# Moving weight splits behind short chains, more room for split weights, and a longer lag of the first layer's down products

## The chip, the cores and the metric

The kernel runs on one core of a Trainium2 chip. The metric is the device time of one execution in microseconds (us). Engines are named as in the profile: PE (TensorE) multiplies matrices, DVE (VectorE) and ACT (ScalarE) work element by element, POOL (GpSimd) and SP (SyncE) do small rest work and issue DMAs.

## The reference

A decoder trunk of two layers on one sequence of 256 tokens, width 1024, all in float32:

```python
for i in range(2):
    h = rms_norm(x, norm_mix_g[i])
    x = x + (nsa_mixer(h, ...) if i == 0 else diff_mixer(h, ...))
    h = rms_norm(x, norm_ffn_g[i])
    u = conv3(h @ ffn_w_up[i]) + ffn_conv_b[i]        # causal, per channel; 1024 -> 2 x 2816
    gate, val = split(u)
    x = x + (silu(gate) * val) @ ffn_w_down[i]        # 2816 -> 1024
return rms_norm(x, final_norm_g)
```

`nsa_mixer` is a sparse attention with 16 heads in 4 groups. K and V of 32-token blocks are compressed by a small network, `gelu(blocks @ w1) @ w2`; each head mixes three softmaxes (over the compressed blocks, the selected blocks and a window) by gates, and an output product with `nsa_w_out` follows. `diff_mixer` has 8 heads with two softmaxes each, `p0 - lam * p1`, a norm per head and the output product.

## The kernel before, in words

**Weights.** Every weight is read once. The host lays them out as units of 128 x 1024 (or 1120) float32 in the order of use. `Stream.load` (L76) brings one to three units in one DMA on SP into a `raw` tile (three buffers). `Stream.split` (L94) makes of each unit a high part `hi`, cast on ACT (L113), and a rest `lo = raw - hi` on DVE (L116). A product is three matmuls: hi by x-high, hi by x-low and lo by x-high, where x itself is split into `xhi` and `xlo` (L186, L187). Split units live in a pool of six (`spl`), or in a place named by `S.place`. `S.fill(n)` splits ahead until n units are ready, `S.next()` takes one. So the 199 splits are background work on ACT and DVE that must stay ahead of PE, and they share these two queues with the short chains of the layers.

**Order.** The text of the kernel gives each engine's instructions, and the framework's scheduler settles the order within each engine's queue. An engine runs its queue in that order; one that waits holds up those behind it. `keep_in_program_order` pins an instruction, which `S.pin` did for one fill.

**First attention, `nsa` (L270).** K, V and q projections, `kbuild` (L467, key casts into the tiles `KK`, `KK2`), `blocks` (L371, the block diagonal of the compression), `cmp_mm` (L395, compression's first product into `cm`), then `cmp_out` (L406), a generator in four steps: copy `hs` on ACT (L409); transposes `ph`, copy `hx` (L415); GELU in `h` (L418 to L421); product `pk` (L441), for K (0) and for V (1). Then a loop over eight pairs of heads: `scores` (L541) with row minima, exponentials and scaling of `p` on DVE (L606), the next q projection, `transposes` (L617, tiles `ta`, `tw`, copies `va`, `vw`), `pv` (L634). The output product `oproj` (L667) runs in pieces; its last piece ends in `residual` (L265): add to `xT`, split into `xhi` and `xlo`, square.

**FFN, `ffn` (L889), twice.** 22 pairs of units: `up(p)` (L944, 48 matmuls into `u`), `conv(p)` (L964: scale `us`, two shifted sums, silu, product, split into `hh` and `hl`, L980 and L982), and `down(p - LAG)` (L922, into `acc`) two pairs behind. `norm_stats` (L204) gives the norm's factors; its diagonal `dg` feeds a small product.

**Second attention, `diff` (L723).** Per head `s_scores`, `s_trans`, `s_pv` and `s_out`, which ends in `doh` (high part on ACT, L829; low part on DVE, L830), read by the output product `dop`.

The change touches `group_plan` (L52), `Stream.split`, `split_tile`, `norm_stats`, `residual`, `nsa`, `diff`, `ffn` and the units' order in the host's packing.

## Time and profile before

| | |
|---|---|
| median of 3 runs | 661.22 us (661.07 to 662.81) |
| the profiled execution's own time | 662.8 us |
| its span in the trace | 661.0 us |
| mean granted clock of PE | 0.992 |
| matmuls on PE | 5026 |
| weights and other reads from memory | 109.27 MB |

The span runs from the first to the last instruction in the trace; the execution's own time holds 1.8 us more around it. Busy time of an engine is the time in which the trace shows it at work. A wait is idle time of an engine, put down to the instruction that ended it.

### The profile page before, as it was taken

To read this page: it belongs to the slowest core of one execution; us is meant where nothing else is said; L and a number is where in the kernel's file an instruction comes from. 1 tells how busy PE (TensorE), PEld (TensorE's weight loads), DVE (VectorE), ACT (ScalarE), POOL (GpSimd) and SP (SyncE) were. 2 spreads that over 40 slices of the span, in tenths; PEclk is the share of its full clock that TensorE was granted. 3 is DMA by queue.
4 is the path that set the end of the run, shared out by engine and by line. 5 is a ranking of instruction groups with operands and counts; after the bars stand their busy time and mean duration, and the time that the engine had idled before them with its cause. 6 is when DMAs were issued, how large, how long until landed. Compare 5 with 4: busy or idle time off the path is not lost.

```text
span 661.0 us, 12566 instructions
## 1 busy us (share of the span) xinstructions
PE 641.6 (97%) x5026; PEld 612.2 (93%) x5026; DVE 513.7 (78%) x990; ACT 413.8 (63%) x818; POOL 27.6 (4%) x39
## 2 busy tenths in 40 slices
PE   8999899999999999999999999999999999999994
PEld 8989798989999999999998899989999999999993
DVE  6899799859867777788859479865987777779664
ACT  7698787658655555567636568645665555558343
POOL 3200000000000000000002000000100000000002
PEclk9999799999999999999999999999999999999998
DMA  8967211124554555546622645720855554555301
GB/s 306 284 252 281 102 65 64 64 97 181 202 190 178 180 178 176 178 178 243 231 89 100 243 152 172 258 97 13 306 191 192 192 190 172 183 180 182 114 1 64
DMA packets 15770, 111.12 MB, mean 168 GB/s; under 512 B 1976, under 2 KB 3512, under 8 KB 5976
## 3 DMA queue, kind: packets, MB, share of 16 engines
q1 hardware_dynamic: 14976, 109.43, 46.5%
q8 instruction: 39, 0.64, 0.4%
q0 software_dynamic: 448, 0.37, 0.3%
q10 hardware_dynamic: 288, 0.52, 0.2%
q14 instruction: 19, 0.16, 0.1%
HBM read 109.27 MB, written 1.05 MB: 167 GB/s over the span
## 4 chain that ended last, share of the span: by engine, by line
PE 61%; issue 24%; DVE 8%; ACT 2%; POOL 1%; DMA 1%; SPq 1%; POOLq 0%; ACTq 0%; DVEq 0%
PE u L954 35%; PE acc L938 10%; PE acc L918 9%; PE dv L247 3%; DVE lo L116 3%; PE dqk L236 2%; PE dop L236 2%; ACT dp L263 1%; DMA raw<-wts 1%; DVE dp L789 1%; POOL dssq L816 1%; DVE dp L262 0%; DVE dp L788 0%; DVE cv L973 0%; DVE dos L820 0%
## 5 line engine op out<-in xcount | busy, mean ns | idle before, releaser
L113 ACT CAST hi<-raw 128x1024 fp32r<-128x1024 f32 (+2 forms) x199 | 202.4, 1045 | 98.6 <-PE u L954 55.8
L116 DVE TENSOR_TENSOR lo<-raw,hi 128x1024 fp32r<-128x1024 f32 (+2 forms) x199 | 239.6, 1222 | 14.5 <-ACT hi L113 14.0
L954 PE MATMUL u<-xhi,lo 128*128 128x256 f32 x704 | 198.6, 282 | 0.0
L954 PE MATMUL u<-xlo,hi 128*128 128x256 f32 x704 | 197.7, 281 | 0.9 <-DVE xlo L187 0.9
L954 PE MATMUL u<-xhi,hi 128*128 128x256 f32 x704 | 198.5, 282 | 0.0
L954 PEld LDWEIGHTS u<-xlo,hi 128*128 128x128 f32 x704 | 132.7, 188 | 1.8 <-DVE xlo L187 1.1
L954 PEld LDWEIGHTS u<-xhi,hi 128*128 128x128 f32 x704 | 132.7, 189 | 0.8 <-ACT xhi L186 0.2
L954 PEld LDWEIGHTS u<-xhi,lo 128*128 128x128 f32 x704 | 132.5, 188 | 0.0
L973 DVE SCALAR_TENSOR_TENSOR cv<-us,cs,cv 128x255 f32<-128x255 f32 (+1 forms) x176 | 74.6, 479 | 4.2 <-ACT cv L971 3.7
L966 DVE TENSOR_TENSOR us<-u,rrs 128x512 f32<-128x512 f32 x44 | 30.4, 690 | 53.4 <-PE u L954 53.3
L971 ACT ACTIVATE cv<-us,cs 128x256 f32<-128x256 f32 x88 | 48.1, 593 | 13.4 <-DVE us L966 13.3
L938 PE MATMUL acc<-hl,hi 128*128 128x256 f32 x176 | 49.7, 283 | 1.1 <-DVE hl L982 1.1
L938 PE MATMUL acc<-hh,lo 128*128 128x256 f32 x176 | 49.7, 282 | 0.0
L938 PE MATMUL acc<-hh,hi 128*128 128x256 f32 x176 | 49.6, 282 | 0.0
L980 ACT CAST hh<-cv 128x256 fp32r<-128x256 f32 x44 | 17.8, 406 | 44.3 <-DVE cv L978 44.3
L236 PE MATMUL dqk<-xhi,hi 128*128 128x256 f32 x128 | 37.1, 290 | 0.0
L236 PE MATMUL dqk<-xhi,lo 128*128 128x256 f32 x128 | 36.0, 282 | 0.0
L236 PE MATMUL dqk<-xlo,hi 128*128 128x256 f32 x128 | 36.0, 281 | 0.0
L938 PEld LDWEIGHTS acc<-hl,hi 128*128 128x128 f32 x176 | 33.2, 189 | 1.3 <-DVE hl L982 1.3
L938 PEld LDWEIGHTS acc<-hh,hi 128*128 128x128 f32 x176 | 33.3, 189 | 0.0
L938 PEld LDWEIGHTS acc<-hh,lo 128*128 128x128 f32 x176 | 33.3, 189 | 0.0
L976 ACT ACTIVATE cv<-cv 128x256 f32<-128x256 f32 x44 | 18.4, 417 | 20.6 <-DVE cv L973 20.6
(242 smaller groups left out, 1266.3 us busy)
## 6 DMA issues: line engine op xcount, KB each, us to landing
raw<-wts SPq DMA_DIRECT2D x40, 1536.0 KB, 6.6
raw<-wts SPq DMA_DIRECT2D x34, 1024.0 KB, 5.0
raw<-wts SPq DMA_DIRECT2D x7, 512.0 KB, 4.8
raw<-wts SPq DMA_DIRECT2D x2, 1120.0 KB, 7.8
db<-bib SPq DMA_DIRECT2D x8, 192.0 KB, 3.6
xT<-xin SPq DMA_DIRECT2D x4, 256.0 KB, 4.3
raw<-wts SPq DMA_DIRECT2D x2, 256.0 KB, 4.1
tail<-fng SPq DMA_DIRECT2D x1, 512.0 KB, 6.5
```

Source lines behind the costliest of these rows:

```text
L113: cast = nc.scalar.copy(hi[:, q], r[:, q])
L116: nc.vector.tensor_tensor(lo[:, q], r[:, q], hi[:, q].bitcast(F32), op=OP.subtract)
L236: nc.tensor.matmul(dst, w[:, kt * P : (kt + 1) * P], x[:, kt, :], start=kt == 0 and i == 0, stop=kt == KT - 1 and i == 2, skip_group_check ...
L247: nc.tensor.matmul(dst, x[:, kt, q * P : (q + 1) * P], w[:, k * cols : (k + 1) * cols], start=kt == 0 and i == 0, stop=kt == KT - 1 and i ...
L918: nc.tensor.matmul(acc[q][c // 512][:, c % 512 : c % 512 + d - c], x[:, qs], w[:, c:d], start=p == 0 and i == 0, stop=p == NPAIR - 1 and i ...
L938: nc.tensor.matmul(acc[dt // 2][:, dt % 2, :], w[:, dt * P : (dt + 1) * P], x, start=p == 0 and i == 0 and dt % 2 == 0, stop=p == NPAIR - ...
L954: nc.tensor.matmul(ps[:, b, :], w[:, kt * P : (kt + 1) * P], x[:, kt, :], start=kt == 0 and b == 0 and i == 0, stop=kt == KT - 1 and i == ...
L966: nc.vector.tensor_tensor(us, ps, rr.unsqueeze(1).to_broadcast([P, 2, T]), op=OP.mult)
L971: nc.scalar.activation(cv[:, b, :], us[:, b, :], AF.Identity, bias=w[3], scale=w[2])
L973: nc.vector.scalar_tensor_tensor(cv[:, b, sft:], us[:, b, : T - sft], w[2 - sft], cv[:, b, sft:], op0=OP.mult, op1=OP.add)
L976: nc.scalar.activation(cv[:, 0, :], cv[:, 0, :], AF.Silu)
L980: nc.scalar.copy(hh, h)
```

## The change

Five things change together.

- `with tc.issue_after(ins):` ties the instructions that a block traces on the engine of `ins` behind `ins` in that engine's queue, without a semaphore. Such blocks hold splits, key builds and `blocks(1)` behind the copies `hs` of the compression, behind its last GELU instruction, behind the last scaling of `p`, behind the last `xlo` of the residuals, and behind the norm's last `dg`. `S.pin` goes.
- Unit order: the second q unit comes ahead of the first unit of the compression of V, and `qproj(1)` in one piece ahead of `cmp_mm(1, 0)`.
- Room: the halves of `xhi` and `xlo` (`spare_x`) hold two units of the output product of each attention when x isn't read any more, and the four `ql` tiles, now one tile `ql4`, hold a unit of the first FFN.
- Order of the last output products: (3, 4, 0, 1, 2) and (4, 5, 0, 1, 2, 3) in place of ascending.
- `LAG` becomes (3, 2): the first layer's down products run three pairs behind.

```diff
@@ -28,3 +28,3 @@
 UW = 1120
-LAG = 2
+LAG = (3, 2)
 LOOK = 3
@@ -54,6 +54,6 @@
     plan += [[1024, 1024]] * 8
-    ffn = [[1024, 1024]] * LAG + [[1024, 1024, 1024]] * (NPAIR - LAG) + [[1024]] * LAG
-    plan += ffn
+    ffn = [[[1024, 1024]] * n + [[1024, 1024, 1024]] * (NPAIR - n) + [[1024]] * n for n in LAG]
+    plan += ffn[0]
     plan += [[1024, 1024]] * 4 + [[1024, 1024]] * 8 + [[1024, 1024]] * 4
-    plan += ffn
+    plan += ffn[1]
     return plan
@@ -74,3 +74,2 @@
         self.place = {}
-        self.pin = None
 
@@ -112,5 +111,3 @@
             q = slice(i * c, (i + 1) * c)
-            cast = nc.scalar.copy(hi[:, q], r[:, q])
-            if self.pin:
-                self.pin(cast)
+            nc.scalar.copy(hi[:, q], r[:, q])
             nc.vector.tensor_tensor(lo[:, q], r[:, q], hi[:, q].bitcast(F32), op=OP.subtract)
@@ -171,2 +168,5 @@
 
+    def spare_x(i):
+        return lambda: tuple(t[:, 4 * i : 4 * i + 4, :].rearrange("p k t -> p (k t)") for t in (xhi, xlo))
+
     def lam_setup():
@@ -186,3 +186,3 @@
         nc.scalar.activation(xhi[:, kt, :], xT[:, kt, :], AF.Copy, scale=gain(n, kt))
-        nc.vector.scalar_tensor_tensor(
+        return nc.vector.scalar_tensor_tensor(
             xlo[:, kt, :], xT[:, kt, :], gain(n, kt), xhi[:, kt, :].bitcast(F32), op0=OP.mult, op1=OP.subtract
@@ -214,4 +214,4 @@
         for q in range(2):
-            nc.vector.tensor_scalar(dg[:, q, :], ident, rc[:, q : q + 1], None, op0=OP.mult)
-        yield
+            last = nc.vector.tensor_scalar(dg[:, q, :], ident, rc[:, q : q + 1], None, op0=OP.mult)
+        yield last
         ps2 = bank(f"rr{n}")
@@ -266,3 +266,3 @@
         nc.vector.tensor_tensor(xT[:, dt, :], ps, xT[:, dt, :], op=OP.add)
-        split_tile(n, dt)
+        st["low"] = split_tile(n, dt)
         sum_squares(n, st, square(n, dt)[:, 0, :], dt)
@@ -303,3 +303,4 @@
             nc.gpsimd.memset(KK2[64:P].bitcast(F32), 0.0)
-            qls = [ap_.tile([P, 2, T], F32R, name=f"ql{i}") for i in range(4)]
+            ql4 = ap_.tile([P, 4, 2, T], F32R, name="ql4")
+            qls = [ql4[:, i] for i in range(4)]
             for t in qls:
@@ -408,4 +409,3 @@
                 hs = at.tile([CB, T], F32, tag="va", name=f"hs{kv}")
-                nc.scalar.copy(hs, ps[:CB, :T])
-                yield
+                yield nc.scalar.copy(hs, ps[:CB, :T])
                 ph = bank(f"ph{kv}")
@@ -414,4 +414,3 @@
                 hx = at.tile([P, 120], F32, tag="hx", name=f"hx{kv}", bufs=1)
-                nc.scalar.copy(hx, ph[:, :120])
-                yield
+                yield nc.scalar.copy(hx, ph[:, :120])
                 h2 = at.tile([P, 120], F32, tag="h2", name=f"h2{kv}", bufs=1)
@@ -420,4 +419,3 @@
                 nc.scalar.activation(h2, h2, AF.Tanh, scale=0.044715 * math.sqrt(2.0 / math.pi))
-                nc.vector.scalar_tensor_tensor(h2, h2, 1.0, hx, op0=OP.add, op1=OP.mult)
-                yield
+                yield nc.vector.scalar_tensor_tensor(h2, h2, 1.0, hx, op0=OP.add, op1=OP.mult)
                 pk = bank(f"pk{kv}")
@@ -507,3 +505,2 @@
             S.fill()
-            blocks(1)
             vproj(0, 1)
@@ -511,8 +508,6 @@
             ck = cmp_out(0)
-            with tc.high_priority():
-                next(ck)
-            S.pin = tc.keep_in_program_order
-            S.fill()
-            S.pin = None
-            kbuild(0, 0)
+            with tc.issue_after(next(ck).ins):
+                S.fill()
+                kbuild(0, 0)
+                blocks(1)
             qproj(0, 0, 4)
@@ -521,9 +516,9 @@
             next(ck)
-            cmp_mm(1, 0)
             S.fill()
             kbuild(1, 0)
-            qproj(1, 0, 8)
+            qproj(1)
+            S.fill()
+            cmp_mm(1, 0)
             cmp_mm(1, 1)
             S.fill()
-            kbuild(0, 1)
             next(ck, None)
@@ -532,10 +527,11 @@
             S.fill()
+            kbuild(0, 1)
             vproj(1, 1)
             cmp_mm(1, 3)
-            S.fill()
-            kbuild(1, 1)
-            nc.vector.tensor_scalar(gt, gt, 1.0, None, op0=OP.add)
-            nc.vector.reciprocal(gt, gt)
             gv = gt.rearrange("p q (h c) -> p q h c", c=3)
 
+            def gates():
+                nc.vector.tensor_scalar(gt, gt, 1.0, None, op0=OP.add)
+                nc.vector.reciprocal(gt, gt)
+
             oh = ohp.tile([P, 2 * KT * T], F32R, tag="sh", name="oh")
@@ -544,3 +540,3 @@
 
-            ph_, pairs = {}, {}
+            ph_, pairs, scaled = {}, {}, []
 
@@ -605,3 +601,3 @@
                     v = t[:, a : a + c.shape[1] * n].rearrange("p (m n) -> p m n", n=n)
-                    nc.vector.tensor_tensor(v, v, c.unsqueeze(2).to_broadcast([P, c.shape[1], n]), op=OP.mult)
+                    scaled.append(nc.vector.tensor_tensor(v, v, c.unsqueeze(2).to_broadcast([P, c.shape[1], n]), op=OP.mult))
 
@@ -655,2 +651,6 @@
 
+            def spare_ql():
+                t = ql4.rearrange("p a b t -> p (a b t)")
+                return t[:, :1024], t[:, 1024:]
+
             def spare(tag):
@@ -673,2 +673,4 @@
 
+            wo0 = S.n - len(S.ready) + 6
+            S.place = {wo0 + 3: spare_x(0), wo0 + 4: spare_x(1)}
             for k in range(NH // 2):
@@ -676,3 +678,4 @@
                     cv_ = cmp_out(1)
-                    next(cv_)
+                    with tc.issue_after(next(cv_).ins):
+                        S.fill()
                 scores(2 * k)
@@ -680,2 +683,3 @@
                     next(cv_)
+                    gates()
                 if k == 1:
@@ -688,4 +692,4 @@
                     oproj(2, 0, 5)
-                S.fill()
                 if k:
+                    S.fill()
                     transposes(2 * k - 2)
@@ -693,4 +697,6 @@
                 scores(2 * k + 1)
+                behind = ExitStack()
                 if k == 0:
-                    next(cv_)
+                    behind.enter_context(tc.issue_after(next(cv_).ins))
+                    kbuild(1, 1)
                 if k <= 5:
@@ -704,2 +710,3 @@
                 S.fill()
+                behind.close()
                 if k:
@@ -707,8 +714,10 @@
             oproj(3, 0, 6)
-            S.place = {S.n: spare("KK"), S.n + 1: spare("KK2")}
-            S.fill(4)
-            oproj(4, 0, 4)
-            transposes(14)
-            oproj(4, 4, 6)
-            transposes(15)
+            S.place |= {S.n: spare("KK"), S.n + 1: spare("KK2"), S.n + 2: spare_ql}
+            with tc.issue_after(scaled[-1].ins):
+                S.fill(4)
+                oproj(4, 0, 4)
+                transposes(14)
+                oproj(4, 4, 6)
+                transposes(15)
+                S.fill(6)
             for dt in range(5):
@@ -716,5 +725,4 @@
             pv(7)
-            for dt in range(5):
+            for dt in (3, 4, 0, 1, 2):
                 oproj(dt, 7, 8)
-            S.fill(7)
 
@@ -728,3 +736,3 @@
             wo0 = S.n - len(S.ready) + 24
-            S.place = {wo0 + i: dx for i in range(3)}
+            S.place = {wo0 + i: dx for i in range(3)} | {wo0 + 4: spare_x(1), wo0 + 5: spare_x(0)}
             V = ap_.tile([P, 2, D], F32, name="dV")
@@ -876,2 +884,3 @@
             oproj(5, 0, 6)
+            S.fill(5)
             for dt in range(4):
@@ -881,5 +890,4 @@
                 oproj(dt, 6, 7)
-            for dt in range(6):
+            for dt in (4, 5, 0, 1, 2, 3):
                 oproj(dt, 7, 8)
-            S.fill(7)
 
@@ -896,3 +904,3 @@
                     mine[0] -= 1
-                    S.split(fx if 1 < mine[0] < 10 or mine[0] >= 60 else None)
+                    S.split(fx if 1 < mine[0] < 10 or (mine[0] >= 60 if l else 56 <= mine[0] < 59) else None)
                 if l == 0 and not mine[0]:
@@ -902,4 +910,7 @@
                 oproj_rest(dt)
-                if dt < KT - 2:
-                    fill(6)
+                if dt == KT - 2:
+                    with tc.issue_after(st["low"].ins):
+                        fill(5)
+            held = ExitStack()
+            held.enter_context(tc.issue_after(st["low"].ins))
             acc = []
@@ -999,3 +1010,4 @@
             nst = norm_stats(2 * l + 1, st)
-            next(nst)
+            held.close()
+            held.enter_context(tc.issue_after(next(nst).ins))
             fill()
@@ -1008,6 +1020,8 @@
             for p in range(2, NPAIR):
+                if p == 4:
+                    held.close()
                 up(p)
                 conv(p)
-                if l == 0 or p < NPAIR - 2:
-                    down(p - LAG, S.next())
+                if p >= LAG[l] and (l == 0 or p < NPAIR - 2):
+                    down(p - LAG[l], S.next())
                 if l and p % 2 and 3 <= p < 11:
@@ -1016,3 +1030,3 @@
                     fill(4 + max(0, min(5, p - 15)))
-            for p in range(NPAIR - 2 * LAG if l else NPAIR - LAG, NPAIR - 1 - l):
+            for p in range(NPAIR - 2 * LAG[l] if l else NPAIR - LAG[l], NPAIR - 1 - l):
                 down(p, S.next())
@@ -1120,3 +1134,3 @@
     units = units[:4]
-    units += kk[:3] + [w1[0][0], kk[3], w1[0][1]] + av[0] + [w1[0][2], w1[0][3], q[0], w1[1][0], q[1], w1[1][1]] + av[1]
+    units += kk[:3] + [w1[0][0], kk[3], w1[0][1]] + av[0] + [w1[0][2], w1[0][3], q[0], q[1], w1[1][0], w1[1][1]] + av[1]
     units += [w1[1][2], w1[1][3]] + q[2:]
@@ -1127,5 +1141,5 @@
         up, dn = i["ffn_w_up"][l], i["ffn_w_down"][l]
-        order = [(p, p - LAG) for p in range(NPAIR)] + [(NPAIR, p) for p in range(NPAIR - LAG, NPAIR)]
+        order = [(p, p - LAG[l]) for p in range(NPAIR)] + [(NPAIR, p) for p in range(NPAIR - LAG[l], NPAIR)]
         if l == 1:
-            order[NPAIR - 2 : NPAIR] = [(NPAIR - 2, -1), (NPAIR - 1, NPAIR - 2 - LAG), (NPAIR, NPAIR - 1 - LAG)]
+            order[NPAIR - 2 : NPAIR] = [(NPAIR - 2, -1), (NPAIR - 1, NPAIR - 2 - LAG[l]), (NPAIR, NPAIR - 1 - LAG[l])]
         for u, d in order:
```

On ACT around the copy `hs` of K's compression, the queue before (`hi` are weight splits, `KK` and `kh` key casts, `C` the block diagonal, `qe` q casts, `h` the GELU's tanh):

```order
L389 CAST CCt<-C_553 128x8x60 x2
L478 CAST kh_736<-k_372 64x256
L490 ACTIVATE Vs<-v_562,rc_247 128x256
L491 ACTIVATE gt<-v_562,nrc 128x24
L409 COPY hs_597<-cm_444 122x256
L113 CAST hi_601<-raw_599 128x1024
L113 CAST hi_666<-raw_599 128x1024
L415 COPY hx_629<-ph_626 128x120
L113 CAST hi_672<-raw_670 128x1120
L113 CAST hi_726<-raw_670 128x1120
L366 CAST qe_645<-qs_643 64x256
```

And of the change:

```order
L410 COPY hs_585<-cm_441 122x256
L112 CAST hi_589<-raw_587 128x1024
L473 CAST KK<-k_369 64x256
L478 CAST KK_147<-k_369 64x256
L473 CAST KK<-k_369 64x256
...
L390 CAST CCt<-C_601 128x8x60 x2
L415 COPY hx_626<-ph_623 128x120
L367 CAST qe_642<-qs_640 64x256
L368 CAST qe_642<-qs_640 64x256
L367 CAST qe_642<-qs_640 64x256
L368 CAST qe_642<-qs_640 64x256
L112 CAST hi_654<-raw_587 128x1024
```

The two casts of V's block diagonal (`CCt`) stood ahead of `hs`; now they, a split and five key casts stand behind it, and the next split (`hi_654`) behind four `qe` casts.

On DVE from the scaling of the first pair's `p` to that of the second pair, before (`lo` are weight splits, `mx` row minima, `ls` sums):

```order
L606 TENSOR_TENSOR p_913<-p_913,ls_870 128x512
L116 TENSOR_TENSOR lo_1282<-raw_1279,hi_1281 128x1024
L631 COPY vw_1025<-tw_1016 128x384
L575 TENSOR_REDUCE mx_1053<-x_1040 128x2
L576 TENSOR_REDUCE mx_1053<-x_1040 128x2
...
L600 TENSOR_SCALAR ls_974<-ls_974 128x12
L601 RECIPROCAL ls_974<-ls_974 128x12
L368 TENSOR_TENSOR ql_162<-qs_1084,qe_1086 64x256
L602 TENSOR_TENSOR ls_974<-ls_974,gt 128x12
L606 TENSOR_TENSOR p_971<-p_971,ls_974 128x256
```

And of the change:

```order
L602 TENSOR_TENSOR p_898<-p_898,ls_857 128x512
...
L113 TENSOR_TENSOR lo_953<-raw_836,hi_952 128x1024
L369 TENSOR_TENSOR ql_159<-qs_943,qe_945 64x256 x2
L113 TENSOR_TENSOR lo_1009<-raw_1006,hi_1008 128x1024
L627 COPY vw_1022<-tw_1013 128x384
L571 TENSOR_REDUCE mx_1050<-x_1037 128x2
L572 TENSOR_REDUCE mx_1050<-x_1037 128x2
L579 TENSOR_REDUCE mx_1050<-w_1038 128x2
L573 TENSOR_TENSOR pc_970<-x_1037,mx_1050 128x64
L361 TENSOR_TENSOR qs_1081<-q_993,rneg 128x256
L113 TENSOR_TENSOR lo_1143<-raw_1006,hi_1142 128x1024
...
L602 TENSOR_TENSOR p_968<-p_968,ls_971 128x256
```

One split stood between the two scalings; now three do, two of them ahead of the copy `vw` and the third behind the next minima.

On DVE at the end of the second attention, around `doh` of the sixth head, before (`dls` sums, the reciprocal among them, `ISA` the score's mask and minimum):

```order
L116 TENSOR_TENSOR lo_5786<-raw_5783,hi_5785 128x1024
L262 ISA dp_5512,dmx_5513<-ds_5515,db_5510 128x128
...
L262 ISA dp_5512,dmx_5513<-ds_5522,db_5510 128x256
L262 ISA dmx_5513 128x1
L785 RECIPROCAL dls_5514<-dls_5514 128x4
L786 TENSOR_SCALAR dls_5514<-dls_5514,nlam 128x2
L830 SCALAR_TENSOR_TENSOR doh<-dpt_5535,gsub,doh 128x256
```

And of the change:

```order
L113 TENSOR_TENSOR xlo<-raw_5591,xhi 128x1024
L262 ISA dp_5505,dmx_5506<-ds_5508,db_5503 128x128
...
L262 ISA dp_5505,dmx_5506<-ds_5515,db_5503 128x256
L262 ISA dmx_5506 128x1
L113 TENSOR_TENSOR xlo<-raw_5591,xhi 128x1024
L793 RECIPROCAL dls_5507<-dls_5507 128x4
L113 TENSOR_TENSOR lo_5704<-raw_5701,hi_5703 128x1024
L794 TENSOR_SCALAR dls_5507<-dls_5507,nlam 128x2
L838 SCALAR_TENSOR_TENSOR doh<-dpt_5528,gsub,doh 128x256
```

Here one weight split stood ahead of `doh`; now there are two splits of a unit into `xlo` and one into the pool.

## Rows read from the trace of the kernel before

**Rows 1.** Page, part 1: busy time (share of the span) and instructions of each engine.
```profile
PE 641.6 (97%) x5026; PEld 612.2 (93%) x5026; DVE 513.7 (78%) x990; ACT 413.8 (63%) x818; POOL 27.6 (4%) x39
```

**Rows 2.** Waits of PE by line: us in total, times, longest us.
```profile
PE pk L441 <- DVE h L421: 2.7, 1, 2.7
PE ph L413 <- ACT hs L409: 1.6, 1, 1.6
PE acc L938 <- DVE hl L982: 1.1, 1, 1.1
...
PE u L954 <- DVE xlo L187: 0.9, 1, 0.9
PE ta L624 <- DVE p L606: 0.9, 3, 0.5
...
PE dop L236 <- ACT doh L829: 0.5, 1, 0.5
```

**Rows 3.** Windows: length, busy time per engine, PEclk, DMA share, GB/s.
```profile
37.00:62.00 25.00, 23.45 (x192) 23.25 (x191) 24.02 (x41) 23.61 (x46) 0.00 (x0) 1.00 0.71 252
44.00:47.00 3.00, 1.45 (x13) 1.25 (x12) 2.86 (x8) 2.95 (x7) 0.00 (x0) 1.00 0.65 273
62.00:115.00 53.00, 49.34 (x424) 45.97 (x423) 47.21 (x127) 41.44 (x137) 0.00 (x0) 0.94 0.28 101
71.30:77.10 5.80, 5.77 (x34) 5.57 (x35) 4.17 (x10) 3.68 (x14) 0.00 (x0) 0.50 0.56 181
178.00:405.00 227.00, 226.40 (x1811) 220.10 (x1812) 172.16 (x294) 132.99 (x212) 6.10 (x6) 1.00 0.49 174
```

**Rows 4.** Timeline of ACT: start us, us, instruction, count, idle before.
```profile
43.76 1.09 ACT L389 CAST CCt<-C 128x480 fp32r<-128x480 f32 x2 [0.69 <-DVE C L379]
...
45.84 0.37 ACT L409 COPY hs<-cm 122x256 f32<-122x256 f32 x1
...
47.98 0.28 ACT L415 COPY hx<-ph 128x120 f32<-128x120 f32 x1
...
50.23 0.41 ACT L366 CAST qe<-qs 64x256 fp32r<-64x256 f32 x1
```

**Rows 5.** Page, part 5: the two splits of a weight unit.
```profile
L113 ACT CAST hi<-raw 128x1024 fp32r<-128x1024 f32 (+2 forms) x199 | 202.4, 1045 | 98.6 <-PE u L954 55.8
L116 DVE TENSOR_TENSOR lo<-raw,hi 128x1024 fp32r<-128x1024 f32 (+2 forms) x199 | 239.6, 1222 | 14.5 <-ACT hi L113 14.0
```

**Rows 6.** Timeline of DVE, ahead of the GELU of V.
```profile
65.55 1.22 DVE L116 TENSOR_TENSOR lo<-raw,hi 128x1024 fp32r<-128x1024 f32 x1
...
68.86 0.69 DVE L583 TENSOR_REDUCE mx<-w 128x2 f32<-128x512 f32 x1
...
69.78 1.22 DVE L116 TENSOR_TENSOR lo<-raw,hi 128x1024 fp32r<-128x1024 f32 x1
...
70.99 0.29 DVE L421 SCALAR_TENSOR_TENSOR h<-h,hx 128x120 f32<-128x120 f32 x1
```

**Rows 7.** Timeline of DVE, ahead of the fifth head pair.
```profile
106.81 1.21 DVE L116 TENSOR_TENSOR lo<-raw,hi 128x1024 fp32r<-128x1024 f32 x1
...
108.27 1.22 DVE L116 TENSOR_TENSOR lo<-raw,hi 128x1024 fp32r<-128x1024 f32 x1
```

**Rows 8.** Timeline of DVE, at the first FFN's first hl.
```profile
176.99 1.22 DVE L116 TENSOR_TENSOR lo<-raw,hi 128x1024 fp32r<-128x1024 f32 x1
178.12 0.42 DVE L982 TENSOR_TENSOR hl<-cv,hh 128x256 fp32r<-128x256 f32 x1
```

**Rows 9.** Timeline of DVE, end of the second attention.
```profile
440.36 0.18 DVE L785 RECIPROCAL dls<-dls 128x4 f32<-128x4 f32 x1 [1.03 <-ACT dp L263]
```

**Rows 10.** Timeline of DVE, start of the second FFN.
```profile
462.54 3.49 DVE L116 TENSOR_TENSOR lo<-raw,hi 128x1024 fp32r<-128x1024 f32 x3
...
466.62 1.22 DVE L116 TENSOR_TENSOR lo<-raw,hi 128x1024 fp32r<-128x1024 f32 x1
467.75 0.48 DVE L187 SCALAR_TENSOR_TENSOR xlo<-xT,cs,xhi 128x256 fp32r<-128x256 f32 x1
```

## The prediction

> **What bounds the kernel now.** I read the busy shares first. TensorE (PE) is busy for 641.6 of 661.0 us [rows 1], so nothing that leaves its matmuls alone can win more than the 19.4 us that it stands idle. The change leaves them alone: PE runs the same 5026 matmuls. Some idle time is fixed, before the first inputs and behind the last matmul, and the change touches neither.
>
> The list of waits then names the rest [rows 2]. The largest single one, 2.7 us, is the second-layer product of the compression of V (`pk`) waiting for the GELU's result on VectorE (DVE). Behind it stand `ph` on the copy `hs` of ScalarE (ACT) with 1.6, the first down product `acc` on `hl` with 1.1, `u` on `xlo` with 0.9, the transposes `ta` on the scaled `p` with 0.9, and `dop` on `doh` with 0.5.
>
> The windows tell which stages have room [rows 3]. From 178 to 405 us, in the first FFN, PE is busy 226.4 of 227 and DVE only 172: what happens there is hidden. In 37 to 62 us DVE is busy 24.0 and ACT 23.6 of 25: there the splitters are as full as PE. From 71.3 to 77.1 us the granted clock is 0.50, which is the 1.2 GHz level; it begins as the wait of 2.7 us for `pk` ends. The idle of 1.55 us inside 44 to 47 (3.00 less 1.45 busy), the wait for `hs`, left the clock at 1.00. PE was busy 5.77 us at half rate, so at full rate the same work takes half: **the low clock costs 2.9 us**, more than the wait itself.
>
> The timelines give the cause of each wait. Just ahead of the last GELU instruction (L421, at 70.99) stands a split that started at 69.78, so it takes 1.2 us of the queue [rows 6]. Two splits stand at 106.8 and 108.3 [rows 7], ahead of the head pair whose transposes wait three times, 0.9 in all [rows 2]; pairs with one or no split show next to none. One stands ahead of `hl` [rows 8], and four (three in one row, one behind them) between the residuals of the second attention and the `xlo` that `u` wants [rows 10]. A wide split costs 1.05 on ACT and 1.22 on DVE, 199 of each [rows 5]. The change only moves them.
>
> **The parts, one by one.** All figures are changes against the profiled execution, 662.8 us by its own time.
>
> A. *The copy `hs0` and the front (37 to 62 us).* The block behind `hs0` takes key builds, the block diagonal casts and a split off ACT's queue ahead of it. `hs0` then waits for `cm` alone, and the wait of 1.6 goes. But they all come right behind it now. Before, `hs` ended at 46.2 [rows 4], so PE stood ready for `ph` at 44.6; a matmul takes 0.125 (227 us over 1811 [rows 3]), 12 of `q` lie between `cm` and `ph`, so `cm` ended at 43.1 and `hs0` (0.37) can end at 43.5. Behind it stand two hi splits of 1.05 [rows 5], five key casts (as the qe casts, 0.41), two CCt casts together 1.09, hx 0.28 and four qe casts of 0.41 [rows 4]: 7.2 us, so the split that `cm1` needs is cast at 50.7. PE comes there after 40 matmuls (`ph` and `q`), 44.6 + 5.0 = 49.6, and waits about 1.1. By the same walk the next two units make it wait about 0.9 and 1.2 more, since the qe casts of the second q unit now stand ahead. Bounds: -1.6 if the splits are not missed, 3.2 - 1.6 = +1.6 if all three waits come. ACT and DVE are 94 and 96% full in this stretch and their work is unchanged, so what leaves one place of their queues is missing at another: I take 0.
>
> B. *`pk` and the clock (68 to 77 us).* The split ahead of L421 leaves (1.2). The one that started at 65.55, between the first two GELU products, moves ahead of both, where it delays them in part; a row maximum of 0.69 comes later than before [rows 6]. The wait of 2.7 becomes 2.7 - 1.2 = 1.5 if the earlier split still counts in full, and 2.7 - 2.4 = 0.3 if not at all; I take 1.0, so -1.7. The trace kept the clock over an idle of 1.55 and lost it over 2.7 [rows 2, 3]; 1.0 is nearer the first, so I take the 2.9 as won. Bounds of the wait: -2.4 and -1.2; of the clock: -2.9 and 0. Sum -4.6.
>
> C. *The head pairs (77 to 115 us).* The splits that left B and the front must run somewhere. Before, one stood between most pairs and two ahead of the fifth. Now two stand ahead of `vw` of the first pair and a third behind it, two each ahead of the third and fourth pairs, none ahead of the fifth. Two in a chain cost 0.9, so two such pairs less one is +0.9. The two ahead of `vw` delay the first P times V by up to 2.4; DVE stood idle there before, but in the time that the low clock gave it. Between 0 and 2.4 I take 1.1. Sum +2.0, bounds 0 to +3.3. Farther on, two xlo casts into spare room stand one to a pair, where the trace shows that one is hidden.
>
> D. *First FFN.* Down products come three pairs behind, so the first `hl` is wanted one pair of ups later, 48 matmuls of 0.125 or 6.0 us, and the wait of 1.1 goes: -1.1, with 0 as the other bound. The one more down product at the layer's end is the same matmuls later; room in the pools is paid for by the spare tile, and DVE's slack hides it.
>
> E. *End of the second attention.* `doh` of the sixth head waits on DVE behind two splits more than before: xlo into spare room ahead of the reciprocal, and one lo behind it. Before, DVE stood idle 1.03 for ACT just ahead of the reciprocal [rows 9], which hides one of them. The other, about 1.2 with no idle time over it, I put at 1.0; it lands on `dop`, which already waited 0.5 [rows 2]. +1.0, bounds 0 to +1.2.
>
> F. *Second FFN's start.* With residuals first and splits behind the last xlo, `u`'s wait on `xlo` goes: -0.9. But three splits held until the norm's last `dg` now stand ahead of `us` and `hh`, and the first down product of this layer, still two pairs behind, finds `hh` late by 0.5 to 1.2 in my walk, or not at all. I take +0.5, so -0.4; bounds -0.9 to +0.3.
>
> SP issues the same weight bytes in nearly the same order, one DMA of two units more at the first FFN's start; POOL's fills of four tiles become one. Neither is waited for in [rows 2], so I cost both at nothing: the raw tiles, loaded ahead, cover them, and an uncovered one would show as a wait of ACT's hi on `wts`.
>
> **Sum:** 0 - 4.6 + 2.0 - 1.1 + 1.0 - 0.4 = -3.1. Against 662.8 that is 659.7 for an execution like the profiled one. The median of the runs shown, 661.2, lies 1.6 lower, so the forecast is **658.1 us**.
>
> **Rivals.**
>
> *Everything goes and nothing takes its place.* All waits named go whole: 1.6 + 2.7 + 2.9 + 0.9 + 1.1 + 0.9 = 10.1, so 651.1. For it: DVE is 78% and ACT 63% busy over all [rows 1], so room exists. Against it: the two stages where most of this lies are those with the fullest splitters [rows 3], and the work is moved, not removed. Chance 0.17.
>
> *The waits come back.* A ends at +1.6, C at +3.3 and F at +0.3: -3.1 + 1.6 + 1.3 + 0.7 = +0.5, so 661.7. For it: DVE's 24.0 of 25. Against it: DVE has 5.8 idle us in 62 to 115. Chance 0.18.
>
> *Short waits drop the clock (slower).* The three new waits of A, 3.2 us of idle in some 5, take PE to 1.2 GHz near 52 us, and the wait that is left at `pk`, followed by that at `vw`, does so once more. Price: A +1.6, a low stretch like the old one +2.9, and the 2.9 of B not won: -3.1 + 1.6 + 2.9 + 2.9 = +4.3, so 665.5. It decides if both happen; one alone leaves it at 662.6 or below, within 0.3%. For it: the splitters' queue. Against it: a single 1.55 left the clock alone. Chance 0.17. The Trainium skill, "TensorE: Matmul & The Clock Gate", section "A second HAM failure mode: psum-queue depth-cycling", speaks for this rival: it tells of a kernel in which PE idled for short times between groups of matmuls often enough that its clock swung between the two levels. By that rule the change would trade one long idle for several harmful ones; the trace of before has no such cluster, so it neither agrees nor disagrees.
>
> *The order moves and nothing follows.* If the new edges only fix an order in which ACT and DVE would have been free anyway, 661.2 stays. The listing shows the moves, so only 0.03.
>
> **How the numbers follow.** A measurement of this kernel can tell 0.3%, 2 us: faster is below 659.2, slower above 663.2. The forecast has 0.45 (its own range 655 to 661, from the bounds of C, E and F): 0.36 of it is faster and 0.09 the same. The first rival gives 0.17 faster, the second 0.03 faster, 0.10 the same and 0.05 slower, the third 0.17 slower, the last 0.03 the same. Sums: faster 0.56, same 0.22, slower 0.22. The range reaches down to 651.5 and up to 664.5: about 0.08 of the first rival lies below and 0.11 of the third above.
>
> **What would show it.** Right: `pk`'s wait at or below 1.5 and a granted clock of 1.00 through 80 us; no wait of `ph` on `hs`, `acc` on `hl` or `u` on `xlo`; new waits of `cm` or `v` on splits near 50 us, of about 1 each; `ta` waits at the third and fourth pairs; `dop`'s wait on `doh` near 1.5. Wrong: a clock of 0.50 anywhere beyond the start (the third rival), PE idle below 12 us (the first), or a wait in the first FFN on a weight split, for which I left no term.

## The result and the profile after

| | before | after |
|---|---|---|
| median beside each other, first runs | 661.28 us (4) | 665.50 us (4) |
| again, in `e12_change_again` | 661.14 us (28) | 665.34 us (11) |
| ratio, with 95% interval | | 1.0054 [1.0033, 1.0075] |
| again | | 1.0057 [1.0038, 1.0076] |
| profiled execution: its time, span | 662.8, 661.0 | 664.06, 662.3 |

The change makes the kernel slower by 0.5%, 4.2 us. 658.1 was forecast, in a range up to 664.5. The profiled execution of before is the slowest of its first four, that of after the fastest of its four, so the two traces differ by 1.3 us only. For a usual execution of the changed kernel I use the trace of `e12_change_again` beside it, the same program with no edit: 665.6 us.

The busy time first, the kernel after:

```profile
PE 641.7 (97%) x5026; PEld 610.4 (92%) x5026; DVE 512.9 (77%) x990; ACT 412.9 (62%) x818; POOL 25.7 (4%) x39
```

It is the work of [rows 1]. What changed are the waits. The list of waits of PE after (line waited for, us in total, times, longest), which answers to [rows 2]:

```profile
PE ta L620 <- DVE p L602: 2.6, 8, 0.8
PE pk L439 <- DVE ls L598: 1.4, 1, 1.4
PE dop L236 <- DVE doh L838: 1.1, 1, 1.1
...
PE cm L405 <- DVE lo L113: 0.9, 1, 0.9
PE v L247 <- DVE lo L113: 0.8, 1, 0.8
PE v L247 <- ACT hi L112: 0.8, 1, 0.8
PE op L236 <- ACT oh L649: 0.5, 1, 0.5
PE dop L236 <- ACT doh L837: 0.5, 1, 0.5
PE tw L620 <- DVE vw L627: 0.4, 1, 0.4
```

The waits that the change aimed at are gone or about halved: `ph` on `hs` (1.6), `acc` on `hl` (1.1), `u` on `xlo` (0.9) are gone, `pk` fell from 2.7 to 1.4. In their place stand three in the front (`cm`, `v`, `v`: 2.5), eight of `ta` (2.6, before 0.9) and a new one of `dop` (1.1).

The windows after, two of them those of [rows 3], with PEclk the third figure from the end:

```profile
37.00:62.00 25.00, 22.37 (x177) 21.56 (x177) 21.73 (x34) 20.82 (x40) 0.00 (x0) 1.00 0.62 220
62.00:115.00 53.00, 49.03 (x434) 44.74 (x433) 47.25 (x125) 43.78 (x141) 0.00 (x0) 1.00 0.26 92
...
442.50:445.90 3.40, 3.40 (x17) 3.40 (x18) 1.59 (x6) 0.00 (x0) 0.69 (x1) 0.50 0.94 383
```

Read the third and fourth busy times of the first row. In the same 25 us DVE worked 24.02 before and works 21.73 now, ACT 23.61 and 20.82. The splitters, nearly full before, now stand idle 3.3 and 4.2 us, which is 2.3 and 2.8 more than before. The half clock of [rows 3] at 71 us is gone, and one has come at 442.5, behind the wait of `dop`.

The usual execution has two. Windows of `e12_change_again`:

```profile
55.70:59.10 3.40, 3.40 (x17) 3.40 (x17) 3.34 (x4) 2.16 (x3) 0.00 (x0) 0.50 0.45 116
444.80:448.20 3.40, 3.40 (x19) 3.40 (x17) 0.83 (x4) 0.00 (x0) 0.69 (x1) 0.50 0.78 323
```

PE is busy through both at the 1.2 GHz level, so each costs half of its 3.4 us, 1.7. One begins behind the three waits of the front, the other behind the two of `dop`.

Why the splitters run dry is in the timelines of the kernel after. ACT (start, us, instruction, idle before):

```profile
40.58 0.41 ACT L478 CAST KK<-k 64x256 fp32r<-64x256 f32 x1
42.34 0.48 ACT L488 ACTIVATE Vs<-v,rc 128x256 f32<-128x256 f32 x1 [1.36 <-PE v L247]
42.72 0.27 ACT L489 ACTIVATE gt<-v,nrc 128x24 f32<-128x24 f32 x1
43.29 0.37 ACT L410 COPY hs<-cm 122x256 f32<-122x256 f32 x1 [0.30 <-PE cm L405]
43.55 1.05 ACT L112 CAST hi<-raw 128x1024 fp32r<-128x1024 f32 x1
```

and DVE, which splits what ACT has cast:

```profile
42.24 0.42 DVE L477 TENSOR_TENSOR KK<-k,KK 64x256 fp32r<-64x256 f32 x1
44.64 1.23 DVE L113 TENSOR_TENSOR lo<-raw,hi 128x1024 fp32r<-128x1024 f32 x1 [1.98 <-ACT hi L112]
```

ACT idles for 1.36 us for `v` and 0.30 for `cm`, both of them PE's, since everything else that it could do stands behind `hs`. DVE idles for 1.98 us, since it waits for ACT's held cast. Before, ACT had casts and key builds for that time.

### The profile page after: what moved, and what is told of

Its sections match the earlier page's. It is cut to its first block, busy times and chain, and to the rows that moved or that the text cites. A ratio compares the mean times of both kernels' runs of the same rounds, so it can differ in the third digit from the quotient of the medians.

```text
span 662.3 us, 12552 instructions
## 1 busy us (share of the span) xinstructions
PE 641.7 (97%) x5026; PEld 610.4 (92%) x5026; DVE 512.9 (77%) x990; ACT 412.9 (62%) x818; POOL 25.7 (4%) x39
## 4 chain that ended last, share of the span: by engine, by line
PE 82%; DVE 8%; ACT 6%; issue 2%; DMA 1%; POOL 0%; SPq 0%; POOLq 0%; DVEq 0%; ACTq 0%
PE u L965 38%; PE acc L949 9%; PE acc L929 9%; PE dv L247 3%; PE op L236 3%; PE dop L236 3%; PE dqk L236 3%; DVE lo L113 2%; PE v L247 2%; PE kc L236 2%; PE k L236 2%; ACT p L582 2%; DVE p L602 1%; PE o L646 1%; PE q L236 1%
## 5 line engine op out<-in xcount | busy, mean ns | idle before, releaser
L112 ACT CAST hi<-raw 128x1024 fp32r<-128x1024 f32 (+2 forms) x194 | 197.1, 1044 | 102.4 <-PE u L965 52.2
L113 DVE TENSOR_TENSOR lo<-raw,hi 128x1024 fp32r<-128x1024 f32 (+2 forms) x194 | 233.3, 1222 | 19.9 <-ACT hi L112 19.3
L965 PE MATMUL u<-xhi,lo 128*128 128x256 f32 x696 | 196.4, 282 | 0.0
L965 PE MATMUL u<-xhi,hi 128*128 128x256 f32 x696 | 195.8, 281 | 0.0
L965 PE MATMUL u<-xlo,hi 128*128 128x256 f32 x696 | 195.2, 280 | 0.0
L965 PEld LDWEIGHTS u<-xlo,hi 128*128 128x128 f32 x696 | 131.1, 188 | 0.7
L965 PEld LDWEIGHTS u<-xhi,lo 128*128 128x128 f32 x696 | 131.0, 188 | 0.0
```

The costliest lines, as they stand in the source:

```text
L112: nc.scalar.copy(hi[:, q], r[:, q])
L113: nc.vector.tensor_tensor(lo[:, q], r[:, q], hi[:, q].bitcast(F32), op=OP.subtract)
L965: nc.tensor.matmul(ps[:, b, :], w[:, kt * P : (kt + 1) * P], x[:, kt, :], start=kt == 0 and b == 0 and i == 0, stop=kt == KT - 1 and i == ...
```

## The experiments

Executions of before stand beside those of each run. Before's median there was 661.28 (e1 to e4), 661.60 (e5 to e8), 661.25 (e9 to e11) and 661.14 (e12 to e14), and differences are given against it. The ratio in brackets, with its 95% interval, is the record's own; it is not the quotient of the two medians and differs from it by up to 0.12% (`e7_lag_held_pk`: 0.9999 against 0.9987).

### The front of the first attention

`e2_no_front` takes the whole front back:

```diff
-units += ... q[0], q[1], w1[1][0], w1[1][1]] + av[1]
+units += ... q[0], w1[1][0], q[1], w1[1][1]] + av[1]
-            with tc.issue_after(next(ck).ins):
-                S.fill()
-                kbuild(0, 0)
-                blocks(1)
+            blocks(1)
...
+            with tc.high_priority():
+                next(ck)
+            S.pin = tc.keep_in_program_order
+            S.fill()
+            S.pin = None
+            kbuild(0, 0)
...
```

Not shown are the key builds of the head pairs, the gates and one fill, which it also puts back where they were.

> The changed kernel with the first attention's front as before: unit order, blocks(1), the key builds and the pinned fill behind hs0 as they were; the blocks held behind hs1, h2 and the last scaling stay. Theory: ph waits 1.6 on hs again, the waits of cm and v on splits near 50 us (0.9, 0.8, 0.8) go, the scores begin 1.7 us earlier: 662 to 664. Rival (the front's splits are work that must be done anyway, so the waits only move to the head pairs): 665 to 666.

Measured: 660.56, 0.7 below before (ratio 0.9985 [0.9971, 1.0000]) and 4.9 below the change. **The front alone carries more than the whole loss**, more than either theory said. `e5_no_hold_hs0` takes back only the held block (the second half of that diff, with `blocks(1)` ahead again) and leaves the new order:

> The changed kernel without the block held behind hs0 (the fill, the key build and the block diagonal stand ahead of it again, the fill pinned); the new unit order stays. Theory (holding work behind a copy that itself waits for PE lets ACT and DVE run dry for some 2 us each, and that time is missing when the next units are wanted): the idle of DVE ahead of the split behind hs0 goes, cm and v wait less, and the time comes near that of e2_no_front: 660.5 to 662.5. Rival (the new order with the second q unit ahead of the compression of V is the cause): 664 to 665.5.

`e6_old_unit_order` takes back only the order (the first two lines, with `cmp_mm(1, 0)` ahead of `qproj(1, 0, 8)` again):

> The changed kernel with the units and q projections in the order of before; the block held behind hs0 stays. Theory (holding is the cause): ACT and DVE run dry as in the change, PE waits some 2 us in 45 to 57: 664 to 665.5. Rival (order is the cause): 660.5 to 662.5.

Measured: e5 661.07, 0.5 below its before (0.9995 [0.9973, 1.0017]); e6 662.96, 1.4 above (1.0021 [0.9999, 1.0042]). Together they make a square, in us against before:

| | order as before | new order |
|---|---|---|
| nothing held behind `hs0` | -0.7 | -0.5 |
| block held behind `hs0` | +1.4 | +4.2 |

The order alone costs nothing that shows, the held block costs 2, and the two together 4.9: neither theory had that. The square is not clean, since the first field alone has the key builds and gates of the head pairs back too. Each field has an interval of about 1 to 1.5 us to either side, so the extra of 2.6 over the sum stands on its edge.

That holding is the cause of the idle splitters shows in the timelines. With the new order and nothing held (`e5_no_hold_hs0`) ACT has no such idle, and DVE this one ahead of the same split:

```profile
46.52 1.23 DVE L116 TENSOR_TENSOR lo<-raw,hi 128x1024 fp32r<-128x1024 f32 x1 [0.62 <-ACT hi L113]
```

With the old order and the block held (`e6_old_unit_order`) both are there, as in the change:

```profile
42.66 0.47 ACT L488 ACTIVATE Vs<-v,rc 128x256 f32<-128x256 f32 x1 [1.48 <-PE v L247]
```

```profile
44.95 1.23 DVE L113 TENSOR_TENSOR lo<-raw,hi 128x1024 fp32r<-128x1024 f32 x1 [2.09 <-ACT hi L112]
```

What it does to PE is in the windows 37 to 62 us; `e2_no_front`, then `e5_no_hold_hs0`, then `e6_old_unit_order`:

```profile
37.00:62.00 25.00, 24.57 (x202) 24.36 (x200) 23.96 (x40) 22.84 (x45) 0.00 (x0) 1.00 0.72 254
```

```profile
37.00:62.00 25.00, 24.21 (x197) 24.01 (x197) 22.41 (x39) 21.64 (x45) 0.00 (x0) 1.00 0.74 262
```

```profile
37.00:62.00 25.00, 23.10 (x185) 22.49 (x184) 21.68 (x35) 21.05 (x42) 0.00 (x0) 1.00 0.62 222
```

PE is busy 24.6, 24.2, 23.1, and 22.4 with both. The splitters are less busy in `e5_no_hold_hs0` too (22.4 and 21.6) and PE is not: their idle time counts only where the next split is due behind it. With the block held, PE waits in `e6_old_unit_order` for the held work itself, the block diagonal, instead of the splits:

```profile
PE cm L404 <- DVE CCt L391: 1.4, 1, 1.4
```

In the change that wait is covered, since the second q product stands ahead of `cm`, but four more qe casts then stand in the queue too, and the splits of three units come late (the waits `cm`, `v`, `v` above). Most of the extra over the sum seems to be the clock. Among executions at a mean granted clock of 0.994 the medians are 660.7 (`e2_no_front`, 6 executions), 661.3 (`e5_no_hold_hs0`, 3), 663.1 (`e6_old_unit_order`, 6) and 664.1 (the change, 1): there the order costs 0.6, holding 2.4 and both 3.4. In the traces, none of them with half clock up to there, the first score matmul starts at 60.46, 60.82, 62.51 and 63.19, which nearly adds up too. But one execution of the change at 0.994 is little to go by.

`e10_lag_held_blocks` holds only the block diagonal behind `hs0`, on top of `e3_lag_held` (below):

```diff
-            blocks(1)
             vproj(0, 1)
             cmp_mm(0, 3)
             ck = cmp_out(0)
-            with tc.high_priority():
-                next(ck)
+            with tc.issue_after(next(ck).ins):
+                blocks(1)
```

> As e3_lag_held, with one small piece of the change's front: the block diagonal of V alone behind hs0 (two casts, 1.1 us), the key build and the split left where they were. Theory (what counts is how much is held): ph's wait on hs falls by about 1.1, the split behind comes 1.1 later and is still in time: 658.5 to 659.5. Rival (anything held behind hs0 comes back at the next units): 659.6 to 661.

Measured: 659.79, 1.5 below before (0.9966 [0.9948, 0.9985]); `e3_lag_held` was 1.7 below. No gain over `e3_lag_held`, so the rival stands, but not for its reason. The scheduler answered the small edit with another order of splits in the head pairs, one ahead of the first and three ahead of the second, where before two and one stood:

```profile
PE ta L620 <- DVE p L602: 2.3, 8, 0.7
PE ph L412 <- ACT hs L409: 1.4, 1, 1.4
...
PE pk L438 <- DVE h L419: 0.9, 1, 0.9
```

`pk` waits 0.9 and `ta` 2.3: what one wait gave, the other took. The clock did better: all twelve executions stand at 0.996 or above, of the twelve of `e3_lag_held` two.

### The GELU of V and the head pairs

`e7_lag_held_pk` has `e3_lag_held` and the blocks held behind `hs1` and the GELU's last instruction:

```diff
-                    next(cv_)
+                    with tc.issue_after(next(cv_).ins):
+                        S.fill()
...
-                    next(cv_)
+                    behind.enter_context(tc.issue_after(next(cv_).ins))
```

> As e3_lag_held, with the splits around the GELU of V held behind hs1 and behind its last instruction as in the change, without spare room for the output product. Theory: the wait of pk falls from 2.6 to about 1.3, and two of the three splits then stand ahead of vw and in the next pair's chain, so ta waits more; net -0.5 to +0.5 against e3_lag_held, and fewer low stretches of the clock: 658.5 to 660. Rival (holding pays whole): 657 to 658.

Measured: 660.71, 0.9 below before (0.9999 [0.9977, 1.0022]), 0.8 worse than `e3_lag_held` against its own before. Its waits:

```profile
PE ta L621 <- DVE p L603: 2.7, 10, 0.4
PE ph L412 <- ACT hs L409: 2.5, 1, 2.5
PE pk L438 <- DVE ls L599: 1.3, 1, 1.3
```

`pk` fell from 2.6 to 1.3 as expected, and `ta` rose from 0.9 to 2.7: on DVE three of the splits stand ahead of the second pair's scaling and two each ahead of the third and fourth, as in the change. The gain is more than spent, and the expected 658.5 to 660 was missed, although the clock fell less often, as expected (nine of twelve executions at 0.995 or above, five in `e3_lag_held`).

`e9_lag_held_spare` leaves these splits alone and adds only the spare room (two units of the output product in `xhi` and `xlo`, one in `ql4`, the fills behind the last scaling, the order 3, 4, 0, 1, 2) to `e3_lag_held`:

```diff
+            S.place = {wo0 + 3: spare_x(0), wo0 + 4: spare_x(1)}
...
-            S.place = {S.n: spare("KK"), S.n + 1: spare("KK2")}
-            S.fill(4)
+            S.place |= {S.n: spare("KK"), S.n + 1: spare("KK2"), S.n + 2: spare_ql}
+            with tc.issue_after(scaled[-1].ins):
+                S.fill(4)
```

> As e3_lag_held, and the spare room of the first attention (two units of the output product in xhi and xlo, one FFN unit in the joined ql tile, splits held behind the last scaling, the new order of output products), with no split held at hs0, hs1 or the GELU of V. The head pairs then keep one split each, also ahead of the fifth. Theory: the ta wait of 0.9 there goes, pk's wait of 2.6 stays: 0.9 to 1.5 below e3_lag_held, 658.1 to 658.8, and faster than both kernels. Rival (the splits only move to the pairs that come later): 659.3 to 660.

Measured: 660.07, 1.2 below before (0.9986 [0.9963, 1.0009]); not better than `e3_lag_held`, so the theory falls and the rival stands. No `ta` waits ahead of the fifth pair any more, but ahead of the sixth, where the two splits into `xlo` now stand one behind the other. DVE, and the transposes of PE behind it:

```profile
115.21 2.35 DVE L116 TENSOR_TENSOR xlo<-raw,xhi 128x1024 fp32r<-128x1024 f32 x2
...
119.56 1.02 DVE L610 TENSOR_TENSOR p<-p,ls 128x256 f32<-128x256 f32 x2
```

```profile
120.13 0.30 PE L628 MATMUL ta<-ks__71,p 128*128 128x128 f32 x1 [0.57 <-DVE p L610]
120.64 0.44 PE L628 MATMUL ta<-ks__71,p 128*128 128x128 f32 x2 [0.21 <-DVE p L610]
...
121.87 0.41 PE L628 MATMUL ta<-ks__71,p 128*128 128x128 f32 x2 [0.25 <-DVE p L610]
```

0.57 + 0.21 + 0.25 = 1.0, where the two splits of [rows 7] cost 0.9. `e11_lag_held_spare_blocks` has its edits and those of `e10_lag_held_blocks`:

> e9_lag_held_spare and e10_lag_held_blocks together. Theory: the gains add up, 657.2 to 658.3. Rival: no better than e9_lag_held_spare.

Measured: 659.61, 1.6 below (0.9975 [0.9955, 0.9996]): nothing adds up beyond `e3_lag_held`.

### The end of the second attention

`e1_no_diff` takes it back from the change:

```diff
-            S.place = {wo0 + i: dx for i in range(3)} | {wo0 + 4: spare_x(1), wo0 + 5: spare_x(0)}
+            S.place = {wo0 + i: dx for i in range(3)}
-            S.fill(5)
-            for dt in (4, 5, 0, 1, 2, 3):
+            for dt in range(6):
```

> The changed kernel with the second attention's end as before (no spare room in xhi and xlo there, no fill of five, output products in ascending order). Theory (local waits add up, and each cluster of waits can cost a stretch at half clock): the wait of dop on doh goes from 1.6 back to 0.5 and the granted clock stays at 1.00 near 443 us, so 1.0 to 2.7 us below the changed kernel's 665.5: 662.8 to 664.5. Rival (the clock falls by chance wherever it falls, and the local waits cancel): the low stretch comes elsewhere, 664.5 to 666.

`e4_lag_held_diff` adds it to `e3_lag_held`:

> As e3_lag_held, and the end of the second attention as in the change. Theory: dop waits 1.0 more on doh, and the idle there (1.6 in a microsecond and a half) takes the clock down for 3.4 us, 1.7 more: 1.0 to 2.7 above e3_lag_held. Rival (the new order of output products pays for it by earlier xlo): equal to e3_lag_held within 0.5.

Measured: e1 664.49, 1.0 below the change; e4 660.75, 1.1 above e3. Each difference is small beside its interval (1.0045 [1.0027, 1.0063] and 0.9983 [0.9966, 1.0000]), e1 lies on the border of its theory and its rival, e4 within its theory. The part of the trace of before that [rows 9] does not show, then the timeline of DVE after:

```profile
440.72 0.48 DVE L830 SCALAR_TENSOR_TENSOR doh<-dpt,gsub,doh 128x256 fp32r<-128x256 f32 x1
```

```profile
437.11 1.22 DVE L113 TENSOR_TENSOR xlo<-raw,xhi 128x1024 fp32r<-128x1024 f32 x1
...
439.35 1.22 DVE L113 TENSOR_TENSOR xlo<-raw,xhi 128x1024 fp32r<-128x1024 f32 x1
440.49 0.17 DVE L793 RECIPROCAL dls<-dls 128x4 f32<-128x4 f32 x1
440.57 1.19 DVE L113 TENSOR_TENSOR lo<-raw,hi 128x1024 fp32r<-128x1024 f32 x1
441.69 0.22 DVE L794 TENSOR_SCALAR dls<-dls,nlam 128x2 f32<-128x2 f32 x1
441.82 0.48 DVE L838 SCALAR_TENSOR_TENSOR doh<-dpt,gsub,doh 128x256 fp32r<-128x256 f32 x1
```

The xlo split at 439.35 fills the time in which DVE stood idle before, and the reciprocal is done at the same time (440.49, before 440.36). The split behind it takes its 1.2 us whole, and `doh` starts at 441.82 where it started at 440.72, so `dop` waits 1.1 more. In the trace of `e1_no_diff` the wait of 1.1 and the stretch at 443 are gone, and one stands in the front instead:

```profile
56.20:59.60 3.40, 3.40 (x17) 3.40 (x16) 3.31 (x5) 1.86 (x2) 0.00 (x0) 0.50 0.54 152
```

The wait at `dop` is paid back, as the rival of `e4_lag_held_diff` had it: the second FFN is 0.95 us shorter with this part (188.35 against 189.3, below). At a mean clock of 0.997 `e2_no_front`, which has the part, and `e8_no_front_no_diff`, which has not, are equal (659.4 and 659.6, five executions each). What the part costs is the clock: seven of twelve executions of the first stand at 0.994 or below, two of the second.

### The FFNs

`e3_lag_held` is before with `LAG = (3, 2)` and the splits held at the FFNs' starts; `e13_lag_only` and `e14_held_only` are its halves.

```diff
-LAG = 2
+LAG = (3, 2)
...
+            held = ExitStack()
+            held.enter_context(tc.issue_after(st["low"].ins))
...
+            held.close()
+            held.enter_context(tc.issue_after(next(nst).ins))
```

> The kernel before with two parts of the change alone: down products of the first layer three pairs behind, and splits held behind the last xlo and the last dg at the FFNs' starts. Theory: the wait of acc on hl (1.1) and that of u on xlo (0.9) go and nothing takes their place: 2.0 to 2.8 below 661.3, so 658.5 to 659.3. Rival (u's wait went because of the new order of the last output products, not because of the held splits): only acc's wait goes, 660.0 to 660.3.

> The kernel before with the first layer's down products three pairs behind, nothing else. Theory (term D of the prediction): the wait of acc on hl goes, 1.1 to 1.3 below before: 660.0 to 660.3. Rival (the gain of e3_lag_held came from the held splits): 661.0 to 661.5.

> The kernel before with splits held behind the last xlo and the last dg at both FFNs' starts, nothing else. Theory (term F): u's wait of 0.9 on xlo goes and little takes its place: 0.4 to 1.3 below before, 660.0 to 660.9. Rival (hh comes late for the first down product): 661.2 to 661.7.

Measured against before: e3 659.62, -1.7 (0.9974 [0.9961, 0.9987]), e13 659.37, -1.8 (0.9974 [0.9954, 0.9995]), e14 660.23, -0.9 (0.9982 [0.9964, 1.0000]). The waits say which half does what. `e13_lag_only` keeps `u`'s wait and has none of `acc`; `e14_held_only` the other way round, with 0.3 of `acc` left:

```profile
PE u L954 <- DVE xlo L187: 0.9, 1, 0.9
```

```profile
PE acc L941 <- DVE hl L985: 0.3, 1, 0.3
```

So each part removes its own wait, and holding takes most of that of `acc` too. Their sum is not resolved against `e3_lag_held` by the times: e13 lies below its theory's 660.0, but seven of its twelve executions stand at a mean clock of 0.997 and one of 28 of before. `e3_lag_held` missed its theory's 659.3 by 0.3. It beats both kernels, and so does `e8_no_front_no_diff`, which takes the diffs of `e2_no_front` and `e1_no_diff` together from the change:

> The changed kernel with both the first attention's front and the second attention's end as before. Theory (parts add up): e2_no_front less what e1_no_diff won against the change, 1.0: 659.5, the same as e3_lag_held within 0.5, since the gain at pk is spent on the ta waits of the head pairs. Rival (the parts hang together): 660.5 or more.

Measured: 659.62, 2.0 below before (0.9976 [0.9956, 0.9995]), like `e3_lag_held`. Here the parts do add up.

### Waiting or clock

> The changed kernel once more, unaltered, with twelve executions beside as many of before, so that its times can be sorted by the mean granted clock of each execution. Theory (waits and clock both cost): its executions at the highest clock lie 2 to 3 above those of before at the highest clock, and it has more executions at a lower clock, which makes the medians 3 to 4.5 apart. Rival (clock alone): at equal clock the two kernels agree within 1.

The executions of that run, sorted by mean granted clock (count, median us; a lower mean means more time at half clock):

```
clock    before        after
0.997     1  659.5
0.996     3  658.7
0.995     4  661.1
0.994    16  661.2      1  664.1
0.993                   1  664.0
0.992     3  662.5      5  665.6
0.991                   4  665.2
0.987     1  666.5
```

At 0.994 the two kernels are 2.9 apart, at 0.992 3.1: these parts are waiting. The usual execution of before is at 0.994, that of after at 0.991 or 0.992, which is worth 1.4. Only two executions of after stand at 0.993 or 0.994, so this split is rough, and before's fastest executions, at 0.995 to 0.997, have no counterpart: at each kernel's own highest clock, as the theory was put, the two are 4.6 apart.

The traces give a second one. PE runs the same matmuls in each stage, so the time between the first matmuls of two stages can be compared between kernels (us; * with half clock in it, 6.8 us of it before, 3.4 after). `e13_lag_only` has before's order outside the first FFN and a trace at full clock, `e5_no_hold_hs0` the change without the block behind `hs0`, also at full clock:

| stage of PE | before | `e13_lag_only` | `e5_no_hold_hs0` | after |
|---|---|---|---|---|
| to the first score matmul | 61.45 | 62.01 | 60.82 | 63.19 |
| head pairs, to the first up product | 97.88* | 95.24 | 97.81 | 97.52 |
| first FFN, to the second attention | 213.62 | 212.33 | 212.32 | 212.35 |
| second attention, to its FFN's first up product | 89.60 | 89.53 | 90.40 | 91.94* |
| second FFN, to the last matmul | 189.78 | 189.82 | 188.35 | 188.34 |

Without the clock the change costs 1.7 in the front (1.2 against `e13_lag_only`, whose `ph` waits 2.1) and 2.3 in the head pairs (97.5 against 95.2), wins 1.3 in the first FFN, and loses 0.9 and wins 1.5 in the last two stages: +2.1 in all. The theory holds in this form: **2 to 3 of the 4.2 us are waits, the rest is the clock**.

## Why the prediction was wrong

*A, the front: the first step that failed.* The prediction took 0, since the queues were full and "what leaves one place of their queues is missing at another". The waits named came nearly as walked (0.9, 0.8 and 0.8; forecast about 1.1, 0.9 and 1.2), but the rule for the sum was false: held work is not moved to another place of a full queue when the instruction that it stands behind itself waits for PE. The queue empties, and DVE and ACT work 2.3 and 2.8 us less in this stretch. The right value was about the upper bound, +1.6: the first score matmul comes 1.7 later, the kernel before and after:

```profile
61.45 0.31 PE L557 MATMUL x<-mkr,idr 128*128 128x320 f32 x1
```

```profile
63.19 0.31 PE L553 MATMUL x<-mkr,idr 128*128 128x320 f32 x1
```

and 3.4 later in `e12_change_again`, with the low clock:

```profile
64.86 0.31 PE L553 MATMUL x<-mkr,idr 128*128 128x320 f32 x1
```

Taking the front back won 4.9 with the clock.

*B and the clock: the second step that failed.* `pk` waits 1.4 (forecast 1.0) and the clock stays at 1.00 there, as forecast. But -4.6 counted a stretch of half clock as gone for good, and the wait of `pk` did not bring it every time. With the same wait of 2.6 or 2.7 the stretch behind it lasts 6.8 us in the traces of before (5.8 of them with PE at work) and `e14_held_only`, 3.4 in `e4_lag_held_diff` and `e9_lag_held_spare`, and there is none in `e3_lag_held` and `e13_lag_only`. The last one's wait, and its window:

```profile
PE pk L441 <- DVE h L421: 2.7, 1, 2.7
```

```profile
70.00:78.00 8.00, 5.41 (x53) 5.10 (x53) 7.72 (x19) 7.85 (x29) 0.00 (x0) 1.00 0.37 131
```

The changed kernel has its low stretches at 55.7 and 444.8 instead. The forecast also took this loss off twice: 2.9 in B, and most of the 1.6 that lead from the profiled execution to the median, since that execution stands at a mean clock of 0.992 and most others at 0.994 (662.5 and 661.2 in the list above).

*C, and what a wait costs.* `ta` and `tw` together wait 1.9 more (2.6 + 0.4 against 0.9 + 0.2); forecast +2.0. `e9_lag_held_spare` too shows two splits in one pair's chain at about 1.0 of `ta` waits. Yet B and C, by their waits +0.6, make the head pairs 2.3 longer at equal clock. A wait costs more than its idle time. In an unbroken row the matmuls start 0.12 apart while each is shown for 0.28; behind a wait that overlap is lost:

```profile
50.06 0.28 PE L405 MATMUL cm<-lo,CCt 128*61 128x256 f32 x1
50.45 0.38 PE L404 MATMUL cm<-hi,CCt 128*122 128x256 f32 x1
51.72 0.33 PE L405 MATMUL cm<-lo,CCt 128*61 128x256 f32 x1 [0.88 <-DVE lo L113]
```

From 50.45 to 51.72 are 1.27, 1.15 more than 0.12, for an idle time of 0.88. So one long wait turned into many short ones gets dearer. In the front the same reckoning, start to start, gives the 1.7: 3.4 lost with the wait at 50.45 that the list leaves out, less 1.7 won at `ph`. In the head pairs it gives about 2.0 of the 2.3, at 15 places where `e13_lag_only` has 8; the rest stays open.

*D and F.* The waits went, -1.1 and -0.9; forecast -1.1 and -0.4. By the stages they are worth 1.3 and 0.5 (the second FFN lasts 189.3 in `e3_lag_held`). In `e3_lag_held` the first down product comes some 0.3 late behind `hh`, less than the forecast's 0.5; in the change it is not late.

*E.* +1.1, forecast +1.0, but the second FFN gives 0.95 back. That this wait could also take the clock down, which is what it costs, had no term.

*The sum.* Without the clock the listed waits give, in the order A to F, 0.9 - 1.3 + 1.9 - 1.1 + 1.1 - 0.9 = +0.6, the stages +2.1; the forecast's own terms without the clock are -0.2. The rest of the miss is the 2.9 that was not there to win, the 1.6 beside it, and one more low stretch than before in the usual execution.

*The rivals.* The third, short waits that drop the clock, with 665.5, came true in its mechanism and had 0.17. Its first place was right, the second was `dop`, not `pk`. That its number is the measured one is luck: it took 2.9 for each stretch, which cost 1.7, and left the head pairs 2 too short. The rule of the Trainium skill beside it, "TensorE: Matmul & The Clock Gate", section "A second HAM failure mode: psum-queue depth-cycling", agrees with the traces in part: three waits of 0.8 to 0.9 within 5 us went ahead of a stretch at 0.50 at 55.7 us in `e12_change_again`, while the first trace of the change has the same waits and no such stretch. That it takes several is not shown. In `e3_lag_held`, with the front of before, `ph` waited 1.8 in the profiled execution, and a stretch at 0.50 came behind it:

```profile
48.00:51.40 3.40, 3.40 (x18) 3.40 (x17) 3.37 (x6) 3.37 (x6) 0.00 (x0) 0.50 0.04 7
```

A wait of `ph` of 2.5 in `e7_lag_held_pk` had one behind it too, those of 2.0 and 2.1 in `e4_lag_held_diff` and `e13_lag_only` had none. So the point against this rival, that a single 1.55 left the clock alone, was one execution's luck, and the length of a wait alone does not decide.
